# Retention's value and gate projections with 512 moving weight columns instead of 256, two heads to a tile

## The chip, the cores and the metric

One core of a Trainium2 chip runs the whole program. The metric is device time in microseconds (us), the median of the timed runs; lower is better. TensorE (PE in the profile) multiplies, VectorE (DVE), ScalarE (ACT) and GpSimd (POOL) do the elementwise work, and SyncE (SP) issues most of the transfers. Every engine takes its instructions in the order in which they were laid down; a waiting instruction holds up everything behind it on its engine.

## The reference

A trunk of four layers works on 384 token columns: 128 context tokens and 256 sample tokens, model width 1024. Layers 0 and 3 are S5 state-space layers, layer 1 is bidirectional retention, layer 2 is Hyena. The change is in layer 1:

```
proj = h @ w_in                       # h (L, 1024), w_in (1024, 6144)
q, k, v, gate = jnp.split(proj, [RET_QK, 2 * RET_QK, 2 * RET_QK + RET_V], axis=-1)
...                                   # 8 heads: q, k of 128, v and gate of 256 columns each
o = o * lax.rsqrt(jnp.mean(o * o, axis=-1, keepdims=True) + EPS)
out = (o.reshape(bsz, L, RET_V) * jax.nn.silu(gate.astype(F32))).astype(h.dtype) @ w_out
```

## The kernel before

**Split matmuls.** Every large projection is computed as three matmuls: both operands are split into a high and a low part (`hh`, `hl` of the activations, `wh`, `wl` of the weights), and `mm` (L135 to L139) adds hh·wh, hh·wl and hl·wh into one PSUM tile `psd`. There are three such tiles (pool `pd`), one PSUM bank of 512 float32 columns each. The weights come as slabs of 1 MB (tile `wr`, two buffers, `weight`, loaded by SP at L153) and are split piece by piece by `unit` (L157 to L165): ACT rounds a piece of 128x1024 to `wh` (L162), and DVE or POOL subtracts to get `wl` (L149 or L134; in retention every third piece goes to POOL). There are two buffers each of `wh` and `wl`. One such piece is called a unit below.

**Retention, layer 1.** It goes over four pairs of heads (`hp`). For a pair, q and k of both heads are projected with the weights stationary in the array and 384 token columns moving. Values v and gates g are projected the other way round by `tokmajor`: the activations (three blocks of 128 tokens, eight blocks of the model width) are stationary and 256 weight columns, one head's, move. A chunk (v or g of one head) is one slab, two units, 72 matmuls, and it accumulates in all three `psd` tiles at once, in the first 256 columns of each bank. When a token block is done, ACT copies v out of PSUM (L1084), or ACT and DVE make silu(g) (L531, L532). Between the chunks stand the parts of a head: `scores` (q·k, L1013 to L1024), `values` (L1029 to L1053: attention times v, the state, the norm, the product with the gate into `zt` at L1047, the new state) and `turn` (L1059: `zt` transposed for the output projection). `tick()` between them takes one piece of background work: tables for the S5 layer 3 (`gen_b1`, `gen_b2`, `gen_cs`: lines L629 to L676), which use DVE, POOL, PE, ACT and transfers.

**What sets the order.** The order on each engine is fixed before the run: the tile layer's scheduler takes the program's order and its own estimates and lays down one list per engine. A changed chunk therefore moves instructions on all engines and also, a little, in the layers behind it.

**Layer 3, at the end,** takes tables back from memory: `toeplitz` loads a tile `Tt` (two buffers) with eight transfers from SP (L850), PE transposes it (L855). SP's list also holds the loads of adaLN weights (`in_mod_w`) and of the GLU's weights (`in_s_w_glu`, L153), in the order laid down.

Of the kernel before, what the change touches and what calls it, by code (L numbers as in the profile page):

```python
# [10 lines left out]
F32 = mybir.dt.float32  # L11
# [6 lines left out]
D = 1024  # L18
NB = D // 128
# [11 lines left out]
DV = 256  # L31
# [74 lines left out]
def hybrid_trunk(ctx: ExitStack, tc: tile.TileContext, I, O, dbg=None, layers=(0, 1, 2, 3)):  # L106
    nc = tc.nc
    V, S, G, TE = nc.vector, nc.scalar, nc.gpsimd, nc.tensor
# [27 lines left out]
    def mm(out, lhs, rhs, start=True, stop=True):  # L136
        combos = [(0, 0)] if len(lhs) == 1 else [(0, 0), (0, 1), (1, 0)]
        for i, (a, b) in enumerate(combos):
            TE.matmul(out, lhs[a], rhs[b], start=start and i == 0, stop=stop and i == len(combos) - 1)  # L139
# [11 lines left out]
    def weight(src):  # L151
        raw = wraw.tile(list(src.shape), F32, tag="wr", name="wr")
        nc.sync.dma_start(raw, src)  # L153
        return raw

    def unit(ap):
        if not SPLIT:  # L157
            return [ap]
        a, b = ap.shape[1], ap.shape[2]
        hi, lo = [wsp.tile([128, 1024], F32R, tag="w" + q, name="w" + q)[:, :a * b].rearrange("p (a b) -> p a b", a=a)  # L160
                  for q in "hl"]
        S.copy(hi, ap)  # L162
        sub_any(lo, ap, hi.bitcast(F32))
        return [hi, lo]
# [20 lines left out]
                       k0 + kb == 0, k0 + kb == nkb - 1)  # L185
            epi(base + m, ps[:, :T])

    def tokmajor(raw, act, epi):
        pss = [psd() for _ in range(3)]
        for k0 in range(0, NB, 4):  # L190
            w = unit(raw[:, k0:k0 + 4, :])
            for t in range(3):
                for kb in range(4):
                    mm(pss[t][:, :256], [p[:, k0 + kb, t * 128:(t + 1) * 128] for p in act],
                       [p[:, kb, :] for p in w], k0 + kb == 0, k0 + kb == NB - 1)
        for t in range(3):
            epi(t, pss[t][:, :256])

    def dense(wsrc, nslab, act, nkb, epi, nt=1):
        for s in range(nslab):  # L200
# [152 lines left out]
    def tick(n=1):  # L353
        for _ in range(n):
            if bg:
                bg.popleft()()
# [172 lines left out]
    def silu2(out, ps):  # L529
        th = t384("silu")[:, :ps.shape[1]]  # L530
        S.activation(th, ps, AF.Tanh, scale=0.5)  # L531
        V.scalar_tensor_tensor(out, th, 1.0, ps, op0=OP.add, op1=OP.mult)  # L532
# [400 lines left out]
    def retention(i, zpool, hpool, nxt):  # L933
        es = ExitStack()
        pool = es.enter_context(tc.tile_pool(name="ret", bufs=1, reuse_waits="tile"))
        rot = es.enter_context(tc.tile_pool(name="retr", bufs=2, reuse_waits="tile"))
        h = adanorm(i, hpool)
# [10 lines left out]
        def t1(n):  # L948
            return pool.tile(sh1, F32, name=n)
        ax, e, w, w2, p, lg = t1("ax"), t1("le"), t1("lwq"), t1("lw2"), t1("lp"), t1("lg")  # L950
# [25 lines left out]
        W = I["ret_w_in"]  # L976
# [87 lines left out]
        for hp in range(4):  # L1064
            qk, vg = {}, {}
            heads = [head(2 * hp + m, m, qk, vg) for m in range(2)]

            def qk_chunk(nm, m, raw):
                def epi(_, ps):
                    o = rot.tile([128, T], F32, tag=nm + str(m), name=nm)  # L1070
                    r0 = 0 if nm == "q" else 2
                    sw = rot.tile([128, NLAT], F32, tag="rsw", name="rsw", bufs=1)
                    V.stream_shuffle(sw, ps[:, NCTX:T], [(q + 16) % 32 for q in range(32)])
                    V.tensor_mul(o[:, NCTX:], ps[:, NCTX:T], rope[:, r0, :])
                    S.activation(o[:, :NCTX], ps[:, :NCTX], AF.Copy, scale=1.0 if nm == "q" else 128 ** -0.5)  # L1075
                    gstt(sw, sw, rope[:, r0 + 1, :], OP.mult)
                    gstt(o[:, NCTX:], o[:, NCTX:], sw, OP.add)
                    qk[nm, m] = o
                firstmajor(i, raw[:, :, m * 128:(m + 1) * 128], h, epi, (0 if nm == "q" else 2) + m if hp == 0 else 9)

            def vg_chunk(nm, m):
                o = vg[nm, m] = rot.tile([128, 3, DV], F32, tag=nm, name=nm)
                tokmajor(weight(W[(8 if nm == "v" else 16) + 2 * hp + m]), h,
                         lambda t, ps: S.copy(o[:, t, :], ps) if nm == "v" else silu2(o[:, t, :], ps))  # L1084

            for n, sl in (("q", hp), ("k", 4 + hp)):
                raw = weight(W[sl])
                for m in range(2):
                    qk_chunk(n, m, raw)
                    if late:  # L1090
                        late.pop(0)()
                    tick()
            if hp == 0:
                z += [zblock(zpool, F32) for _ in range(16)]
            vg_chunk("v", 0)
            heads[0][0]()
            tick()
            vg_chunk("g", 0)
            heads[1][0]()
            tick()  # L1100
            vg_chunk("v", 1)
            heads[0][1]()
            tick()
            vg_chunk("g", 1)
            heads[0][2]()
            tick()
            late = [heads[1][1], heads[1][2]]
# [289 lines left out]
    hp = pool_of(eh, "hp")  # L1397
# [12 lines left out]
    for fb in range(NB):  # L1410
        t = xT[:, fb, :]
# [71 lines left out]
def _slabs(w, cols):  # L1483
    k, n = w.shape
    return w.reshape(k // 128, 128, n // cols, cols).transpose(2, 1, 0, 3)


def _layout(a):
    ca = np.ascontiguousarray
    o = {}  # L1490
    x = np.concatenate([a["x_prompt"][0], a["x_sample"][0]], 0)
    o["xT"] = x.T.reshape(NB, 128, T).transpose(1, 0, 2)
    o["condT"] = np.stack([a["c_ctx"], a["c"][0]]).reshape(2, NB, 128).transpose(2, 1, 0)
    o["vec"] = np.concatenate([
        a["mod_b"].reshape(-1, 128), a["norm_g"].reshape(-1, 128), a["final_g"].reshape(-1, 128),
        a["s5_b_glu"].reshape(-1, 128), a["hy_conv_w"].reshape(-1, 128), a["hy_conv_b"].reshape(-1, 128),
        a["hy_skip"].reshape(-1, 128)], 0).T
    o["mod_w"] = np.stack([_slabs(a["mod_w"][i], 256) for i in range(DEPTH)])

    def lanes(re, im):  # L1500
        v = np.stack([re, im], 0)
        v = v.reshape(2, 128, 4, 16, *v.shape[4:])
        return np.moveaxis(v, (2, 0, 3), (0, 1, 2)).reshape(128, 128, *v.shape[4:])
    lam, bc, h0, ds = [], [], [], []
    for j in range(2):
        lr, li = a["s5_lam_re"][j], a["s5_lam_im"][j]
        ls = np.broadcast_to(a["s5_log_step"][j].reshape(1, 128), (128, 128))
        lam.append(np.stack([lanes(lr, lr), lanes(li, li), ls], 1))
        br, bi = a["s5_b_re"][j], a["s5_b_im"][j]
        bl = np.stack([lanes(br, bi), lanes(bi, br)]).reshape(2, 128, 2, 16, 4, 16)  # L1510
        cr, ci = np.swapaxes(a["s5_c_re"][j], 2, 3), np.swapaxes(a["s5_c_im"][j], 2, 3)
        cl = np.stack([lanes(cr, ci), lanes(ci, cr)]).reshape(2, 128, 2, 16, 4, 16)
        v = np.stack([bl, cl]).reshape(2, 2, 128, 2, 4, 4, 4, 16)
        bc.append(v.transpose(4, 2, 5, 0, 3, 1, 6, 7))
        h0.append(lanes(a["state_s5"][0, j, :, 0], a["state_s5"][0, j, :, 1]))
        d = a["s5_d"][j].reshape(16, 4, 1, 16)
        ds.append(np.broadcast_to(d, (16, 4, 2, 16)).reshape(16, 128).T)
    o["s5lam"], o["s5bc"], o["s5h0"], o["s5d"] = map(np.stack, (lam, bc, h0, ds))
    wi = a["s5_w_in"]
    wi = np.concatenate([wi[..., :D].reshape(2, D, 8, 8, 16).swapaxes(3, 4).reshape(2, D, D), wi[..., D:]], 2)  # L1520
    o["s5_w_in"] = np.stack([_slabs(wi[j], 256) for j in range(2)])
    o["s5_w_glu"] = np.stack([_slabs(a["s5_w_glu"][j], 256) for j in range(2)])
    o["s5_w_out"] = np.stack([_slabs(a["s5_w_out"][j], 256) for j in range(2)])
    w = a["ret_w_in"][0]
    qk = w[:, :2 * D].reshape(D, 16, 2, 2, 2, 16).transpose(0, 1, 2, 4, 3, 5).reshape(D, 2 * D)
    o["ret_w_in"] = _slabs(np.concatenate([qk, w[:, 2 * D:]], 1), 256)
    o["ret_w_out"] = _slabs(a["ret_w_out"][0], 128)
    o["decay"] = np.concatenate([a["ret_decay_logit"][0].reshape(16, 1)] * 2, 0)
    s0 = a["state_ret"][0, 0].reshape(2, HEADS, 2, 2, 2, 16, DV).transpose(1, 2, 4, 3, 5, 0, 6)
    o["s0"] = s0.reshape(HEADS, 128, 2, DV)  # L1530
    o["hy_w_in"] = _slabs(a["hy_w_in"][0], 256)
    o["hy_w_out"] = _slabs(a["hy_w_out"][0], 128)
    o["hy_f_w1"], o["hy_f_w2"] = a["hy_f_w1"][0], a["hy_f_w2"][0]
    o["hy_f_b"] = np.stack([a["hy_f_b1"][0], a["hy_f_b2"][0]], 1)
    o["hy_f_w3"] = a["hy_f_w3"][0].reshape(64, 2, 2, 16, 128).transpose(3, 0, 2, 1, 4)
    return {k: ca(v) for k, v in o.items()}
# [39 lines left out]
```

## Time and profile before

| | |
|---|---|
| median of 3 runs | 1651.68 us (1649.26 to 1652.22) |
| the profiled execution's own time | 1654.23 us |
| its span from first to last instruction | 1652.1 us |
| PE busy | 1460.5 us, 88% of the span |
| DVE, ACT, POOL busy | 1250.0, 693.9, 663.5 us |
| mean granted TensorE clock | 0.942 |

Busy times are sums over instructions; a matmul's recorded duration includes its way through the array, so the distance between the starts of two matmuls is what a stream of them costs. "Idle before, releaser" in a row says how long the engine stood and what ended that.

### The profile page before, as it was taken

The numbers are of one execution on the slowest core, as the hardware profiler recorded it, in microseconds if no ns is written. First come the engines' busy times: TensorE is split into PE (matmuls) and PEld (weight loads), VectorE is DVE, ScalarE is ACT, GpSimd is POOL, SyncE is SP. The second block draws the span as 40 slices with busy tenths as digits, with TensorE's granted clock in tenths as the row PEclk, the third lists the DMA queues.
The fourth block names the chain that finished last, engine by engine and source line by source line (L and its number), as shares of the span: only waits on it lengthen the run. The fifth ranks groups of instructions, "written<-read, shape, count | busy, mean of one in ns | idle before, by whom it ended". The sixth has DMA issues, their size and how long they took to land. (4 is left out here: it accounts for less than half of the span.)

```text
span 1652.1 us, 27609 instructions
## 1 busy us (share of the span) xinstructions
PE 1460.5 (88%) x10370; PEld 1290.5 (78%) x10370; DVE 1250.0 (76%) x2935; ACT 693.9 (42%) x1275; POOL 663.5 (40%) x484
## 2 busy tenths in 40 slices
PE   5878876788689999999979999999999999998796
PEld 3655664577579888889968988989999798777686
DVE  8967996589787777755868988887888863399465
ACT  2444421234324333335445545445454442642453
POOL 2111331315275756551325665556656331131221
PEclk9788897799799999999979999999999999998898
DMA  8488589743645555544333223222321353675531
GB/s 355 137 269 243 144 213 272 223 147 140 229 160 182 183 204 188 186 146 142 129 106 102 97 77 99 100 77 77 105 96 66 132 227 140 191 206 179 167 128 64
DMA packets 107805, 261.39 MB, mean 158 GB/s; under 512 B 28535, under 2 KB 68568, under 8 KB 88088
## 3 DMA queue, kind: packets, MB, share of 16 engines
q1 hardware_dynamic: 80768, 200.12, 37.0%
q0 software_dynamic: 11984, 34.87, 7.6%
q10 hardware_dynamic: 14920, 24.65, 4.1%
q8 instruction: 82, 1.34, 0.3%
q14 instruction: 51, 0.42, 0.1%
HBM read 220.37 MB, written 30.83 MB: 152 GB/s over the span
## 5 line engine op out<-in xcount | busy, mean ns | idle before, releaser
L134 POOL TENSOR_TENSOR wl<-wr,wh 128x1024 fp32r<-128x1024 f32 (+2 forms) x99 | 249.7, 2524 | 313.3 <-ACT wh L162 286.2
L162 ACT CAST wh<-wr 128x1024 fp32r<-128x1024 f32 (+4 forms) x211 | 216.0, 1029 | 314.7 <-PE psd L139 222.3
L139 PE MATMUL psd<-hh,wh 128*128 128x384 f32 x880 | 305.0, 348 | 13.8 <-DVE X L796 5.1
L139 PE MATMUL psd<-hh,wl 128*128 128x384 f32 x880 | 303.4, 345 | 5.4 <-POOL wl L134 3.4
L139 PE MATMUL psd<-hl,wh 128*128 128x384 f32 x880 | 303.9, 345 | 2.7 <-DVE hl L470 2.5
L149 DVE TENSOR_TENSOR wl<-wr,wh 128x1024 fp32r<-128x1024 f32 (+3 forms) x112 | 146.7, 1311 | 72.8 <-ACT wh L162 70.3
L139 PEld LDWEIGHTS psd<-hh,wh 128*128 128x128 f32 x880 | 168.2, 192 | 26.2 <-issue 14.3
L139 PEld LDWEIGHTS psd<-hh,wl 128*128 128x128 f32 x880 | 168.3, 191 | 13.8 <-issue 5.1
L139 PEld LDWEIGHTS psd<-hl,wh 128*128 128x128 f32 x880 | 168.3, 191 | 12.4 <-issue 6.4
L139 PE MATMUL psd<-wh,hh 128*128 128x256 f32 x384 | 111.1, 293 | 3.9 <-ACT k L1075 1.8
L139 PE MATMUL psd<-wl,hh 128*128 128x256 f32 x384 | 110.7, 290 | 4.1 <-DVE wl L149 2.2
L139 PE MATMUL psd<-wh,hl 128*128 128x256 f32 x384 | 109.2, 286 | 0.0
L379 PE MATMUL psn<-wr,sgc 128*32 128x256 f32 x640 | 57.0, 449 | 30.7 <-DMA wr<-in_mod_w_dram 25.5
L630 DVE TENSOR_TENSOR xt<-BI,xc 128x512 f32<-128x512 f32 x52 | 47.2, 911 | 44.9 <-DMA CP<-xt 18.9
L139 PE MATMUL psd<-zb,wh 128*128 128x384 f32 x240 | 80.9, 338 | 0.0
L139 PEld LDWEIGHTS psd<-wl,hh 128*128 128x128 f32 x384 | 74.4, 194 | 6.2 <-DVE wl L149 3.1
L139 PEld LDWEIGHTS psd<-wh,hh 128*128 128x128 f32 x384 | 74.0, 194 | 6.1 <-ACT k L1075 2.3
L634 POOL TENSOR_TENSOR BP<-BP,xt 128x512 f32<-128x512 f32 x32 | 46.7, 1460 | 69.8 <-DVE xt L630 47.8
L139 PEld LDWEIGHTS psd<-wh,hl 128*128 128x128 f32 x384 | 74.4, 194 | 0.1
L630 DVE TENSOR_TENSOR xt<-FI,bc 128x512 f32<-128x512 f32 x64 | 51.8, 809 | 17.8 <-POOL BP L634 9.8
L632 POOL DMA_DIRECT2D CP<-xt x32 | 28.0, 929 | 92.7 <-DVE xt L630 43.6
L634 POOL TENSOR_TENSOR CP<-CP,xt 128x512 f32<-128x512 f32 x32 | 50.1, 1565 | 31.1 <-DVE xt L630 19.5
(385 smaller groups left out, 3890.4 us busy)
## 6 DMA issues: line engine op xcount, KB each, us to landing
wr<-in_mod_w_dram SPq DMA_DIRECT2D x40, 1024.0 KB
wr<-in_hy_w_in_dram SPq DMA_DIRECT2D x32, 1024.0 KB
wr<-in_ret_w_in_dram SPq DMA_DIRECT2D x24, 1024.0 KB
wr<-in_s_w_in_dram SPq DMA_DIRECT2D x16, 1024.0 KB
wm<-in_mod_w_dram SPq DMA_DIRECT2D x8, 1024.0 KB
CP<-xt POOLq DMA_DIRECT2D x32, 256.0 KB, 6.9
Tt<-scratch_kd_dram SPq DMA_DIRECT2D x128, 64.0 KB
wr<-in_s_w_glu_dram SPq DMA_DIRECT2D x8, 1024.0 KB
```

The costliest lines, as they stand in the source:

```text
L134: G.tensor_tensor(out, a, b, op=op)
L139: TE.matmul(out, lhs[a], rhs[b], start=start and i == 0, stop=stop and i == len(combos) - 1)
L149: V.tensor_sub(out, a, b)
L162: S.copy(hi, ap)
L379: TE.matmul(ps[q * 32:(q + 1) * 32, :256], sg[:, kb, 6 - 2 * u:38 - 2 * u], raw[:, kb, :], start=u == 0 and k2 == 0, stop=u == 3 and k2 == 1)
L630: eng.tensor_tensor(t, c2, x[:, 1].unsqueeze(2).to_broadcast([128, 4, 8, 16]), op=OP.mult)
L632: nc.gpsimd.dma_start(out, t, accum_op=OP.add)
L634: add.tensor_tensor(out, out, t, op=OP.add)
```

## The change

`tokmajor` now takes units of two blocks of the model width by 512 weight columns (instead of four by 256), loads its slab itself (half the depth of one 512-column slab, again 1 MB), and fills whole PSUM banks. `vg_chunk` is called once for v and once for g of a pair; its output tile holds both heads (one buffer of 512 columns instead of two of 256). v is copied out in one operation of 512 columns, the gate's silu stays in pieces of 256. The calls of `scores`, `values`, `turn` and `tick` are placed anew around the two chunks: v is projected for both heads before any gate. A host-side layout `ret_w_vg` holds the slabs of 512 columns.

```diff
-    def tokmajor(raw, act, epi):
+    def tokmajor(src, act, epi):
         pss = [psd() for _ in range(3)]
-        for k0 in range(0, NB, 4):
-            w = unit(raw[:, k0:k0 + 4, :])
+        for k0 in range(0, NB, 2):
+            if k0 % 4 == 0:
+                raw = weight(src[:, k0:k0 + 4, :])
+            w = unit(raw[:, k0 % 4:k0 % 4 + 2, :])
             for t in range(3):
-                for kb in range(4):
-                    mm(pss[t][:, :256], [p[:, k0 + kb, t * 128:(t + 1) * 128] for p in act],
+                for kb in range(2):
+                    mm(pss[t], [p[:, k0 + kb, t * 128:(t + 1) * 128] for p in act],
                        [p[:, kb, :] for p in w], k0 + kb == 0, k0 + kb == NB - 1)
         for t in range(3):
-            epi(t, pss[t][:, :256])
+            epi(t, pss[t])
...
-            def vg_chunk(nm, m):
-                o = vg[nm, m] = rot.tile([128, 3, DV], F32, tag=nm, name=nm)
-                tokmajor(weight(W[(8 if nm == "v" else 16) + 2 * hp + m]), h,
-                         lambda t, ps: S.copy(o[:, t, :], ps) if nm == "v" else silu2(o[:, t, :], ps))
+            def vg_chunk(nm):
+                o = rot.tile([128, 3, 2 * DV], F32, tag=nm, name=nm, bufs=1)
+                for m in range(2):
+                    vg[nm, m] = o[:, :, m * DV:(m + 1) * DV]
+
+                def epi(t, ps):
+                    if nm == "v":
+                        S.copy(o[:, t, :], ps)
+                        return
+                    for m in range(2):
+                        silu2(vg[nm, m][:, t, :], ps[:, m * DV:(m + 1) * DV])
+                tokmajor(I["ret_w_vg"][hp + (0 if nm == "v" else 4)], h, epi)
...
-            vg_chunk("v", 0)
             heads[0][0]()
+            vg_chunk("v")
             tick()
-            vg_chunk("g", 0)
             heads[1][0]()
             tick()
-            vg_chunk("v", 1)
+            vg_chunk("g")
             heads[0][1]()
             tick()
-            vg_chunk("g", 1)
             heads[0][2]()
             tick()
```

What the scheduler makes of it is shown at two places. The first is PE's list at the end of the last pair's gate chunk, just before the output projection begins (`zt` is the gated output of a head, `s_...` its cached state, `zhh` the first split input of the output projection). Before:

```order
L139 MATMUL psd<-wh,hl 128x256
L1059 MATMUL psm<-ident,zt 128x128 x5
L1029 MATMUL psm<-v,A 128x256
L1033 MATMUL psm<-s_7880,qf 128x256
L1034 MATMUL psm<-s_7880,qf 128x256
```

And with the change, at the same place:

```order
L139 MATMUL psd<-wh,hl 128x512
L139 MATMUL psd<-zhh,wh 128x384
L1061 MATMUL psm<-ident,zt 128x128 x2
L1031 MATMUL psm<-v,A 128x256
L1061 MATMUL psm<-ident,zt 128x128 x4
L1035 MATMUL psm<-s_7330,qf 128x256
```

The transposes of the pair's first head stood behind a gate that had been ready one chunk earlier; now they stand one or two matmuls behind the last matmul of the gate chunk that makes their gate.

The second place is SP's list in layer 3 (`Tt` are the tables of `toeplitz`, eight transfers a table; `wr` are weight slabs). Before:

```order
L153 DMA wr<-in_mod_w_dram 128x2048
L850 DMA Tt<-scratch_kd_dram 16x8x128 x5
L153 DMA wr<-in_s_w_glu_dram 128x2048 x2
L850 DMA Tt<-scratch_kd_dram 16x8x128 x16
L153 DMA wr<-in_s_w_glu_dram 128x2048 x2
```

And with the change:

```order
L153 DMA wr<-in_mod_w_dram 128x2048
L852 DMA Tt<-scratch_kd_dram 16x8x128
L153 DMA wr<-in_s_w_glu_dram 128x2048
L852 DMA Tt<-scratch_kd_dram 16x8x128 x8
L153 DMA wr<-in_s_w_glu_dram 128x2048
L852 DMA Tt<-scratch_kd_dram 16x8x128 x16
```

The first of the two GLU slabs that stood right before the last two tables (the sixteen transfers) has moved ahead of the table before them.

## Rows read from the trace of the kernel before

**Rows 1.** The page's first line.

```profile
span 1652.1 us, 27609 instructions
```

**Rows 2.** Retention's stage: PE, PEld, DVE, ACT, POOL busy us (instructions); clock; DMA share; GB/s.

```profile
470.00:765.00 295.00, 276.18 (x2055) 255.57 (x2056) 207.48 (x369) 111.38 (x249) 172.06 (x127) 0.98 0.52 176
```

**Rows 3.** Groups of matmuls, retention: one of three alike forms (wl,hh and wh,hl too).

```profile
L139 PE MATMUL psd<-wh,hh 128*128 128x256 f32 x384 | 111.1, 293 | 3.9 <-ACT k L1075 1.8 <-ACT q L1075 1.4 <-DVE g L532 0.7
```

**Rows 4.** PE's waits, 465 to 765 us: total us, times, longest; six of twelve.

```profile
PE psd L139 <- POOL wl L134: 4.1, 5, 1.2
...
PE psd L139 <- DVE g L532: 2.9, 3, 2.2
PE psd L139 <- DVE wl L149: 2.2, 3, 1.0
...
PE psd L139 <- ACT k L1075: 1.8, 2, 0.9
...
PE psm L1059 <- DVE zt L1047: 1.1, 1, 1.1
...
PE psm L1021 <- ACT PB L673: 0.2, 1, 0.2
```

**Rows 5.** PE's timeline inside a chunk: 256 columns, full clock, 68 starts apart.

```profile
741.10 0.28 PE L139 MATMUL psd<-wh,hh 128*128 128x256 f32 x1
...
749.26 0.28 PE L139 MATMUL psd<-wh,hl 128*128 128x256 f32 x1
```

**Rows 6.** PE's timeline in layer 3: 384 columns, full clock, 12 starts apart.

```profile
1584.77 0.33 PE L139 MATMUL psd<-gh,wh 128*128 128x384 f32 x1
...
1586.85 0.33 PE L139 MATMUL psd<-gh,wh 128*128 128x384 f32 x1
```

**Rows 7.** A stretch of low clock (columns as Rows 2), and 256-column starts, nine apart.

```profile
471.00:477.80 6.80, 5.91 (x29) 5.62 (x28) 4.98 (x7) 0.28 (x1) 5.34 (x5) 0.50 0.39 124
...
474.59 0.41 PE L139 MATMUL psd<-wh,hh 128*128 128x256 f32 x1
...
476.51 0.41 PE L139 MATMUL psd<-wh,hh 128*128 128x256 f32 x1
```

**Rows 8.** Groups of ACT, POOL and DVE work, 465 to 765 us.

```profile
L162 ACT CAST wh<-wr 128x1024 fp32r<-128x1024 f32 x45 | 47.2, 1050 | 65.8 <-PE psd L139 54.0 <-DVE nr L279 4.9 <-DVE xt L630 2.4
...
L673 ACT COPY PB<-psm 128x512 f32<-128x512 f32 x28 | 15.6, 593 | 14.0 <-PE psd L139 5.6 <-DVE xt L630 4.1 <-PE psm L672 3.7
L1084 ACT COPY v<-psd 128x256 f32<-128x256 f32 x24 | 8.7, 371 | 17.2 <-PE psd L139 16.4 <-POOL CP L634 0.6 <-issue 0.2
...
L134 POOL TENSOR_TENSOR wl<-wr,wh 128x1024 fp32r<-128x1024 f32 x15 | 37.2, 2480 | 31.8 <-ACT wh L162 31.8
...
L149 DVE TENSOR_TENSOR wl<-wr,wh 128x1024 fp32r<-128x1024 f32 x30 | 42.3, 1410 | 9.5 <-ACT wh L162 9.3
...
L532 DVE SCALAR_TENSOR_TENSOR g<-silu,psd 128x256 f32<-128x256 f32 x24 | 9.5, 413 | 7.2 <-ACT silu L531 7.2
```

**Rows 9.** Timelines of PE and DVE where one pair's gate chunk meets the next pair.

```profile
603.98 0.59 PE L139 MATMUL psd<-hh,wh 128*128 128x384 f32 x1 [2.17 <-DVE g L532]
...
599.40 3.59 DVE L629 TENSOR_TENSOR CP<-B,xc 128x512 f32<-128x512 f32 x2 [1.09 <-DMA scratch_cpd_dram<-CP]
```

**Rows 10.** The chain that ended last, two of its longest pieces: start, us, what.

```profile
1528.71 10.38 DMA Tt<-scratch_kd_dram
1543.01 6.49 DMA Tt<-scratch_kd_dram
```

**Rows 11.** SP's timeline in layer 3.

```profile
1514.46 7.87 SPq L850 DMA_DIRECT2D Tt<-scratch_kd_dram  x5
1522.43 3.10 SPq L153 DMA_DIRECT2D wr<-in_s_w_glu_dram  x2
1526.81 16.79 SPq L850 DMA_DIRECT2D Tt<-scratch_kd_dram  x16
```

**Rows 12.** Layer 3 while the last tables load (columns as Rows 2).

```profile
1525.00:1530.00 5.00, 3.86 (x48) 3.50 (x44) 2.72 (x13) 3.09 (x6) 1.05 (x2) 1.00 1.01 406
```

More of the change, by code (lines that the diff above doesn't have):

```diff
@@ L1525, in _layout @@
     qk = w[:, :2 * D].reshape(D, 16, 2, 2, 2, 16).transpose(0, 1, 2, 4, 3, 5).reshape(D, 2 * D)
-    o["ret_w_in"] = _slabs(np.concatenate([qk, w[:, 2 * D:]], 1), 256)
+    o["ret_w_in"] = _slabs(qk, 256)
+    o["ret_w_vg"] = _slabs(w[:, 2 * D:], 512)
     o["ret_w_out"] = _slabs(a["ret_w_out"][0], 128)
```

## The prediction

> **What bounds the kernel now.** I read the stages first. The layers run one after another, so a microsecond taken from the stage of retention comes off the span [rows 1] unless a later stage waits for something else. In that stage, 295 us long, PE is busy for 276 us, DVE for 207, POOL for 172 and ACT for 111, at a granted clock of 0.98 and with half of the DMA share unused [rows 2]. PE is the bound. The waits of PE confirm it from the other side: the twelve rows of that list add up to 20.3 us, none of them above 4.1 us in total [rows 4]. So what shortens PE's stream shortens the stage, and what can take it back is a wait of PE for a weight part (`wl`), for a PSUM tile that is not yet read out (g, k), or for `zt`.
>
> The stream itself I read from the distances between starts, since recorded durations overlap (293 ns for a 256-column matmul [rows 3] that in fact comes every 120 ns). At full clock, 256 columns: 749.26 - 741.10 = 8.16 us over 68 steps, 120.0 ns each [rows 5]. 384 columns: 2.08 us over 12 steps, 173.3 ns [rows 6]. The 128 columns between them cost 53.3 ns, 0.417 ns a column, which is one column per cycle at 2.4 GHz; what is left is 13.3 ns at 256 columns and 13.3 ns at 384. So a matmul costs its columns and a fixed 13.3 ns. At a clock of 0.50 the fixed part is gone: 1.92 us over nine steps is 213.3 ns, 256 cycles of 1.2 GHz and nothing more [rows 7].
>
> **The change, part by part.**
>
> *The stream.* 3 x 384 = 1152 matmuls of 256 columns [rows 3] become 576 of 512. The columns stay; 576 fixed parts go. No row has 512 columns, so the price of one is drawn along the line of the two rows: 213.3 + 13.3 = 226.7 ns. Some 30 of the 1152 run at low clock, where nothing is saved. 561 x 13.3 ns = **-7.5 us**. Bounds: 0, if 512 columns cost twice what 256 cost (240 ns), and -7.7, if all run at full clock. I take the line because the two rows have the same remainder. The weight loads that go with the 576 lie beside the matmuls and are not counted again.
>
> The Trainium skill, page "TensorE: Matmul & The Clock Gate", section "Wait — 56ns, not 53.3ns?", gives a matmul N/2.4 GHz plus about 2.5 ns when warm; by it the 576 would be worth about 1.4 us, an estimate from that page. The rows here show 13.3 ns and not 2.5, so the trace does not agree.
>
> *The units.* Their number (eight a pair), size and split between DVE and POOL stay. But a unit now lasts 18 x 226.7 ns = 4.08 us on PE instead of 36 x 120.0 = 4.32 us. With two buffers, the unit after next is prepared while one unit runs: 1.05 us of rounding on ACT and 1.41 us on DVE or 2.48 us on POOL [rows 8], 2.5 or 3.5 us without any queue. A DVE unit keeps 1.6 us in hand, a POOL unit 0.55 us, and POOL and DVE also carry the background tables in order. Eight times before, PE waited for `wl` (4.1 us for POOL's, 2.2 us for DVE's) [rows 4]. A unit that is waited for loses its whole 0.24 us. Bounds: 0, and 32 x 0.24 = 7.7 us if every unit is limited by its preparation. I take six units in the stage, **+1.5 us**, because PE's waits for `wl` are few.
>
> *The ends of chunks.* ACT's v copies become 12 of 512 columns; the row for a 512-column copy out of PSUM is 593 ns, against 2 x 371 [rows 8]. That is off the path: with the token blocks outermost in a unit, block 0 is complete 12 x 226.7 ns = 2.7 us before the chunk's end, and its copy is done by then. A gate block now needs two tanh and two products of 413 ns on DVE [rows 8] instead of one before its PSUM tile is free, and the next pair's q chunk takes that tile. Before, PE stood 2.17 us there once, because DVE's list had two background products (3.59 us, they themselves waited for a transfer) ahead of the gate [rows 9]; three such waits cost 2.9 us [rows 4]. Chunk ends fall from four a pair to two, but the one in front of q stays, with one product more. Bounds: -2.9 us if these waits vanish, +1.7 us if all four pairs wait one product more. I take **+0.5 us**.
>
> *The last pair.* PE's list now has the first head's transposes one or two matmuls behind the last gate matmul. They wait for tanh, product and `zt`. The nearest row is the one wait for `zt`, 1.1 us [rows 4]; I take **+1.1 us**, with 0 and 2.2 as bounds (once or twice). Behind it stand the second head's products and the output projection, all on PE. For the other pairs, the q and k chunks stand between, which hide it.
>
> *Layer 3.* Nothing was changed there, but SP's list was. At the end the chain runs through two table loads of 10.38 and 6.49 us [rows 10], issued at 1526.81 us right behind two GLU slabs (2 MB) [rows 11], while the DMA share is 1.01 at 406 GB/s [rows 12]. With the change one slab goes out a table earlier. If it has landed by then, 1 MB at 406 GB/s, 2.6 us, is taken from the queue in front of the tables: -2.6 us. Against it: the eight transfers of the table before now stand between the two slabs. In the group of five before, 7.87 us passed [rows 11], 1.57 us each; if these eight can only start where the first slab stood and go at that rate, the last tables start 12.6 us later: +12.6 us is the other bound. I take **-1.0 us**. The moved rows in Hyena I cost at nothing, without a row that bounds them.
>
> **Sum:** -7.5 + 1.5 + 0.5 + 1.1 - 1.0 = -5.4 us. Against the profiled execution's own 1654.2 us (span 1652.1 us) that is 1648.8 us; its time lies 2.5 us above the median of the runs shown, so against the median of 1651.7 us it is **1646 us**.
>
> **The rivals.**
>
> 1. *More than the stream.* The gate waits vanish (-2.9) and the slab leaves the table loads' way (-2.6), with the unit and `zt` terms near nothing: -7.5 - 5.5 = -13.0, 1638.7 us. For it speaks that half of the chunk ends go; against it that the waits for g came from background work on DVE, which stays.
>
> 2. *The gain is eaten.* PE's stream is shorter, but the preparation of units sets the pace. 32 units that all lose 0.24 us give +7.7 - 7.5, about 1652 us. The same time comes out if the fixed part does not belong to the matmul as such and 512 columns cost 240 ns. For the first speaks that POOL units have only 0.55 us in hand; against it that PE's waits for `wl` were 6.3 us in 295. Against the second speaks the equal remainder of the two rows. The page's 2.5 ns, named above, would end here too.
>
> 3. *Slower, through SP's list in layer 3.* The eight transfers between the slabs start late and go at 1.57 us each, which pushes the last two tables back by 12.6 us, and these end the chain: -7.5 + 1.5 + 0.5 + 1.1 + 12.6 = +8.2, 1659.9 us. It decides once the last tables start more than 7.7 us later, counted from the end of retention (4.4 us to use up the gain, 3.3 to be seen). For it speaks that these transfers wait for one another and for PE today; against it that the slab in front of them is free to go early.
>
> **How the numbers follow.** About 0.2%, 3.3 us, is what a measurement of this kernel can tell from no change. Forecast (3.3 to 9 us faster): 0.47. First rival (over 9 us faster): 0.18. Second (within 3.3 us): 0.21. Third (slower by over 3.3 us, with other new orders that I have not priced): 0.14. So faster 0.65, same 0.21, slower 0.14. The forecast's own range is 1642.5 to 1648.5 us. All bounds together reach from -13.2 us (1638.5) to +16.7 us (1668.4); the lower end stays, and above I cut where the second rival's bound (+4.1 with the other terms at their upper ends but layer 3's) is still held: 1638 to 1656 us.
>
> **What would show it.** The starts of 512-column matmuls at full clock should be 226.7 ns apart; 240 ns would break the first term. Retention's stage should be some 4 to 7 us shorter at the same clock. PE's waits for `wl` should come to some 8 us (6.3 + 1.5). At the end of the last gate chunk PE should show a wait for `zt` of 1 to 2 us. The two table loads in the chain's end should together take less than 16.9 us, and start at the same distance from the end of retention. The prediction is wrong if the stage is shorter by less than 3 us, or if layers 2 and 3 change by more than 3 us.

## The result and the profile after

The changed kernel is slower. Its median is 1670.16 us (1668.57 to 1672.48) beside 1651.05 us (1649.26 to 1652.22) for the kernel before, a ratio of 1.0106 with a 95% interval of 1.0086 to 1.0127, so 14 to 21 us. The profiled execution took 1672.48 us; its page begins:

```profile
span 1670.7 us, 26436 instructions
```

Beside [rows 1] that is 18.6 us more with 1173 instructions fewer. I cut the span at events that both kernels have. In the table, a stage runs from the start of the first v matmul (or g, where g comes first) to the start of the last matmul of the v and g chunks; "behind" is the way from there to the first matmul of Hyena I, layer 2; "rest" is the way from there to the end. A second execution of each kernel (e16 and e13 below) shows how far the pieces repeat.

| profiled execution | first v matmul at | stage | behind | rest | span |
|---|---|---|---|---|---|
| before | 469.3 | 289.5 | 89.8 | 803.5 | 1652.1 |
| before again (e16) | 475.0 | 289.3 | 90.4 | 801.3 | 1655.9 |
| after | 471.7 | 291.6 | 101.7 | 805.8 | 1670.7 |
| after again (e13) | 468.5 | 290.0 | 102.7 | 807.1 | 1668.2 |

Two things went wrong. The stage is not shorter (290.8 us on average beside 289.4; the two executions of after differ by 1.6 us), and 12 us are lost behind it. Some 4 us more stand in the rest, half of them behind the last matmul of layer 3's input projection and half ahead of it. No experiment here isolates these 4 us: in the other versions below, the rest lies between 799.6 and 806.9 us, in those with all four pairs wide between 799.6 and 804.4.

First what came as forecast. PE's timeline inside a chunk, 512 columns, 12 starts apart, answers to [rows 5]:

```profile
750.11 0.39 PE L139 MATMUL psd<-wh,hh 128*128 128x512 f32 x1
...
752.83 0.39 PE L139 MATMUL psd<-wh,hl 128*128 128x512 f32 x1
```

2.72 us over 12 steps is 226.7 ns. The window of retention's stage has the columns of [rows 2]; behind it stand PE's waits from 467 to 767 us, four of fifteen, as in [rows 4]:

```profile
470.00:765.00 295.00, 268.72 (x1449) 217.06 (x1447) 208.81 (x346) 105.30 (x221) 175.82 (x129) 0.98 0.53 176
```

```profile
PE psd L139 <- DVE wl L149: 7.5, 7, 3.4
PE psm L674 <- DVE nr L282: 3.0, 1, 3.0
...
PE psd L139 <- DVE g L534: 2.0, 2, 1.7
...
PE psd L139 <- POOL wl L134: 1.6, 1, 1.6
```

PE is busy for 7.5 us less than in [rows 2], but that is not the stage's own difference: before, the window ends with 6 us of full work behind the stage, after, with PE standing. Between the first and the last start of the chunks PE is busy for 267.6 us after (267.2 in e13) beside 270.4 before (267.5 in e16), and idle for 24.0 us (22.8) beside 19.1 (21.7). So most of the stream's gain is used up while PE is busy, and the waits grow. The waits for `wl` are 9.1 us in place of 6.3, 7.5 of them now for DVE, the longest 3.4 us.

Now the end of the last gate chunk. PE's timeline, with what ended its idle time in brackets:

```profile
763.23 0.39 PE L139 MATMUL psd<-wh,hl 128*128 128x512 f32 x1
764.00 0.45 PE L139 MATMUL psd<-zhh,wh 128*128 128x384 f32 x1 [0.38 <-ACT zhh L245]
773.47 0.69 PE L1061 MATMUL psm<-ident,zt 128*128 128x128 f32 x2 [9.03 <-DVE zt L1049]
773.95 1.06 PE L1031 MATMUL psm<-v,A 128*128 128x256 f32 x2
774.80 1.06 PE L1061 MATMUL psm<-ident,zt 128*128 128x128 f32 x4
...
776.83 0.59 PE L1037 MATMUL psm<-v,A 128*128 128x256 f32 x2
777.26 0.59 PE L1038 MATMUL psm<-v,A 128*128 128x256 f32 x2
...
780.09 0.52 PE L139 MATMUL psd<-zb,wh 128*128 128x384 f32 x1
```

One matmul of the output projection runs, then PE stands for 9.03 us before head 6's transposes; head 7's products are next in the list. What it waits for is seen on ACT and then on DVE:

```profile
763.43 2.16 ACT L245 CAST zhh<-zb 128x384 fp32r<-128x384 f32 x5 [0.51 <-PE psd L139]
765.50 0.64 ACT L533 ACTIVATE silu<-psd 128x256 f32<-128x256 f32 x2
766.04 1.33 ACT L245 CAST zhh<-zb 128x384 fp32r<-128x384 f32 x3
767.27 1.75 ACT L245 CAST zhl<-zb 128x384 fp32r<-128x384 f32 x4
768.92 0.83 ACT L162 CAST wh<-wr 128x768 fp32r<-128x768 f32 x1
769.65 0.38 ACT L533 ACTIVATE silu<-psd 128x256 f32<-128x256 f32 x1
769.92 0.38 ACT L1043 ACTIVATE junk<-psm 128x256 f32<-128x256 f32 x1
```

```profile
770.66 0.41 DVE L534 SCALAR_TENSOR_TENSOR g<-silu,psd 128x256 f32<-128x256 f32 x1
771.15 0.17 DVE L1044 TENSOR_SCALAR rss<-rss 128x3 f32<-128x3 f32 x1
...
772.74 0.16 DVE L286 SCALAR_TENSOR_TENSOR rrs<-nr 128x3 f32<-128x3 f32 x1
772.93 1.27 DVE L1049 SCALAR_TENSOR_TENSOR zt<-psm,rrs,g 128x256 f32<-128x256 f32 x3
```

ACT rounds z for the output projection between the tanhs (12 casts, then a weight cast), so the last tanh starts 6.4 us behind the chunk's last start. Head 6's norm stands behind that tanh on ACT (`junk`) and DVE (`rss` to `rrs`), and only then comes `zt`. PE stands, the granted clock falls to its low level, 0.50, and head 6's transposes and the first of head 7's products run at it: the two products at 773.95 us take 0.85 us to the next start, two later ones (776.83 us) 0.43. Windows of after, columns as [rows 2]:

```profile
760.00:765.00 5.00, 4.07 (x17) 2.84 (x16) 1.78 (x5) 3.20 (x8) 1.95 (x2) 1.00 0.15 52
765.00:770.00 5.00, 0.00 (x0) 0.00 (x0) 0.97 (x3) 5.00 (x14) 0.00 (x0) 0.60 0.00 0
770.00:775.00 5.00, 1.53 (x5) 1.24 (x6) 4.61 (x16) 1.12 (x7) 0.00 (x0) 0.50 0.20 56
775.00:780.00 5.00, 5.00 (x24) 4.47 (x23) 5.00 (x12) 2.54 (x9) 0.00 (x0) 0.87 0.00 0
```

The projection's matmuls run in a row from 780.1 us, 16.9 us behind the last gate matmul. Before, PE was busy throughout from 755 to 790 us at a clock of 1.00, and the distance was 4.4 us. The last gate matmul, the first of the projection, and a window of before:

```profile
758.86 0.29 PE L139 MATMUL psd<-wh,hl 128*128 128x256 f32 x1
...
763.23 0.52 PE L139 MATMUL psd<-zhh,wh 128*128 128x384 f32 x1
```

```profile
760.00:765.00 5.00, 5.00 (x27) 4.59 (x26) 4.99 (x12) 5.00 (x13) 0.00 (x0) 1.00 0.00 0
```

### The profile page after: what moved, and what is told of

Its sections match the earlier page's. It is cut to its first block, busy times and chain, and to the rows that moved or that the text cites. A ratio compares the mean times of both kernels' runs of the same rounds, so it can differ in the third digit from the quotient of the medians.

```text
span 1670.7 us, 26436 instructions
## 1 busy us (share of the span) xinstructions
PE 1455.5 (87%) x9794; PEld 1257.8 (75%) x9794; DVE 1250.0 (75%) x2935; ACT 693.0 (41%) x1263; POOL 669.9 (40%) x484
## 5 line engine op out<-in xcount | busy, mean ns | idle before, releaser
L149 DVE TENSOR_TENSOR wl<-wr,wh 128x1024 fp32r<-128x1024 f32 (+3 forms) x112 | 143.3, 1280 | 72.2 <-ACT wh L162 68.1
L632 DVE TENSOR_TENSOR xt<-BI,xc 128x512 f32<-128x512 f32 x52 | 53.1, 1023 | 42.7 <-POOL CP L636 18.1
L139 PE MATMUL psd<-wl,hh 128*128 128x512 f32 x192 | 79.6, 415 | 5.1 <-DVE wl L149 3.3
L636 POOL TENSOR_TENSOR BP<-BP,xt 128x512 f32<-128x512 f32 x32 | 52.3, 1636 | 65.0 <-DVE xt L632 49.6
L139 PE MATMUL psd<-wh,hl 128*128 128x512 f32 x192 | 76.2, 397 | 0.0
L139 PE MATMUL psd<-wh,hh 128*128 128x512 f32 x192 | 72.6, 411 | 3.1 <-ACT q L1077 1.4
L631 DVE TENSOR_TENSOR BP<-F,bc 128x512 f32<-128x512 f32 x64 | 59.5, 939 | 12.9 <-PE psm L674 10.8
L631 DVE TENSOR_TENSOR CP<-B,xc 128x512 f32<-128x512 f32 x52 | 43.9, 879 | 24.0 <-DMA scratch_cpd_dram<-CP 14.3
L797 DVE TENSOR_TENSOR X<-X,m 128x64 f32<-128x64 f32 x184 | 60.5, 329 | 0.0
L381 PEld LDWEIGHTS psn<-wr,sgc 128*32 128x32 f32 x640 | 19.1, 119 | 54.9 <-DMA wr<-in_mod_w_dram 29.3
```

The source lines that it names most:

```text
L149: V.tensor_sub(out, a, b)
L381: TE.matmul(ps[q * 32:(q + 1) * 32, :256], sg[:, kb, 6 - 2 * u:38 - 2 * u], raw[:, kb, :], start=u == 0 and k2 == 0, stop=u == 3 and k2 == 1)
L631: eng.tensor_tensor(out, c1, x[:, 0].unsqueeze(2).to_broadcast([128, 4, 8, 16]), op=OP.mult)
L632: eng.tensor_tensor(t, c2, x[:, 1].unsqueeze(2).to_broadcast([128, 4, 8, 16]), op=OP.mult)
L636: add.tensor_tensor(out, out, t, op=OP.add)
L797: V.tensor_add(dst, dst, m1[:, 0])
```

## The experiments

Single runs of one kernel spread over up to some 20 us in these comparisons, so beside each ratio I give the stage and "behind" of its profiled execution. Each ratio is to runs of the kernel before that were taken beside it; their medians lie between 1651.5 and 1656.4 us. Theory A names the last gate chunk's end, B the width and background work in the stage, C the list of SP in layer 3 (my third rival). `vg_chunk1` is the chunk of before, one head and 256 columns, but it reads half of a 512-column slab and writes into one tile for both heads.

**Only the last pair old (e1).** The calls, shown joined here, stand on lines of their own.

```diff
+            if hp < 3:
...
+            else:
+                vg_chunk1("v", 0); heads[0][0](); tick()
+                vg_chunk1("g", 0); heads[1][0](); tick()
+                vg_chunk1("v", 1); heads[0][1](); tick()
+                vg_chunk1("g", 1); heads[0][2](); tick()
```

> The changed kernel with only the last of the four pairs done as before: four chunks of 256 columns, v and g of the first head, then v and g of the second. Theory A (the last gate: both heads' gates are now complete only at the end of the last chunk, ACT's last tanh stands behind the rounding for the output projection, and PE's list waits for it): 12.8 us of the 19 come back, 1657 us. Theory B (512 columns slow the stage itself, by units that are waited for and by background work that now falls in bunches between fewer chunks): a quarter of it at most, some 2 us, 1668 us. Theory C (SP's list in layer 3, as my third rival said): no change, 1670 us.

Measured: 1655.75 us, ratio to before 1.0028 (1.0007 to 1.0049); stage 292.5, behind 93.2 us. Theory A holds for what is behind the stage: 9 of the 12 us are back. The three wide pairs that stay bring no gain.

**The counterpart: only the last pair new (e10).** The two branches of e1 exchanged.

> The counterpart of the run with only the last pair old: the first three pairs as before (256 columns, old order), only the last pair with 512 columns and both heads' gates last. Theory A (the end of the last gate chunk): the distance from the last gate matmul to the first matmul of Hyena I is some 12 us longer than before (about 102 instead of 90 us), and the whole 1660 to 1665 us. Theory B (the width within the stage): 1651 to 1654 us.

Measured: 1671.38 us, ratio 1.0102 (1.0073 to 1.0130); stage 287.4, behind 104.7 us. The one pair costs as much as the whole change, 18 us by the medians; 1660 to 1665 us was expected. Its stage is 2.0 us shorter than before, so one wide pair at the end loses nothing within the stage. Its wait for `zt` is that of after:

```profile
PE psm L1072 <- DVE zt L1060: 9.0, 1, 9.0
```

**ACT's rounding behind the last tanh (e2).**

```diff
-        S.activation(th, ps, AF.Tanh, scale=0.5)
+        lastg[0] = S.activation(th, ps, AF.Tanh, scale=0.5)
...
-        op.split(0, 14)
+        with tc.issue_after(lastg[0].ins):
+            op.split(0, 14)
```

> The changed kernel with one edge more: on ACT the rounding for the output projection may not stand ahead of the last tanh of the last gate. Theory A: the last tanh ends at about 764.5 us instead of 770, so the 17.3 us between the last gate matmul and the output projection become some 10 to 12 (the norm's chain and zt still stand between, 4 us), 1663 to 1666 us. If instead the order on ACT does not matter, because the rounding that is moved back is then waited for just as long: 1669 to 1671 us. Theories B and C: no change, 1670 us.

Measured: 1668.39 us, ratio 1.0097 (1.0075 to 1.0120); stage 290.0, behind 98.2 us. The last tanh starts 4 us earlier, at 765.6 us, and 3.5 us come back behind the chunk; the median, 1.8 us lower than that of after, lies within the spread and between the two ranges expected. PE's waits there, 756 to 785 us:

```profile
PE psd L139 <- ACT zhh L245: 4.5, 1, 4.5
PE psm L1063 <- DVE zt L1051: 1.2, 1, 1.2
```

PE now waits for the rounding, which stands behind tanh and norm, and then for `zt`. ACT's order is a part of the loss; moving it alone mostly exchanges one wait for another.

**The norm early as well (e12).**

`values()` is cut in two: `products()`, with the norm, which is entry 3 of a head and is called half way through the last gate chunk, and `zt` behind the chunk.

```diff
-            vg_chunk("g")
+            vg_chunk("g", heads[0][3] if hp == 3 else lambda: None)
...
+        with tc.issue_after(lastg[0].ins):
+            op.split(0, 14)
```

> The changed kernel, in the last pair with the first head's products and norm in the middle of the gate chunk, and on ACT no rounding for the output projection ahead of the last tanh. Between the last gate matmul and the first head's transposes only tanh, product and zt are left. Theory A in its full form (what waits is the chain tanh, product, norm, zt, wherever ACT's rounding stands): the wait for zt falls from 9.0 to about 3 us, the distance from the last gate matmul to Hyena I to 93 to 96 us, 1660 to 1664 us. If that time is lost wherever both heads end together: no change, 1668 to 1671 us.

Measured: 1657.36 us, ratio 1.0028 (1.0004 to 1.0052); stage 291.3, behind 93.1 us, so 9 of the 12 us are back, with both heads' gates still last; that is more than the 1660 to 1664 us expected. On ACT the last tanh now starts at 763.98 us, and on PE the wait has nearly gone:

```profile
764.40 0.44 PE L1070 MATMUL psm<-ident,zt 128*128 128x128 f32 x2 [0.64 <-DVE zt L1064]
```

```profile
765.00:770.00 5.00, 5.00 (x27) 4.61 (x26) 5.00 (x12) 5.00 (x14) 0.00 (x0) 1.00 0.18 52
```

PE stays busy at a clock of 1.00 where it stood at 0.60 in after. So it is the serial chain tanh, product, norm, `zt`, put behind the last chunk together with ACT's rounding, and not the width, that costs the 9 us. The norm early without the change on ACT was not run, so beyond e2's 3.5 us the two shares are not separated.

**The order without the width (e4).** `vg_chunk1("v", 0)` and `("v", 1)` at the place of the wide v chunk, g likewise; matmuls and units of 256 columns.

> The changed kernel's order and pair tiles (v of both heads, then g of both heads, background work and head work at the same places), but with matmuls of 256 columns and units of 4 x 256 as before. If the order is the cause (theory A and the bunches of theory B): the loss stays and the 7.5 us of the stream go too, 1672 to 1678 us. If the width is the cause (units of 512 columns that are waited for): back to 1651 to 1656 us.

Measured: 1669.76 us, ratio 1.0112 (1.0079 to 1.0146); stage 293.0, behind 96.7 us. By the median the loss stays without the width, a little under the lower end that was expected, so the order is enough for a loss. But the profiled execution was the fastest of its runs (1659.45 us), and it shows only 6.7 of the 12 us behind the stage. There the first head's gate is complete one chunk of 256 columns earlier, ACT has two casts ahead of the last tanh in place of twelve, and PE's wait is shorter:

```profile
PE psm L1072 <- DVE zt L1060: 3.5, 1, 3.5
```

Its stage is 3.6 us longer than before, with 5.1 us of waits for ACT's copies of v, where two v chunks now follow each other.

**g first (e6), and g first with all head work later (e9).**

```diff
-            vg_chunk("v")
+            vg_chunk("g")
...
-            vg_chunk("g")
+            vg_chunk("v")
```

In e9, also `values` and `turn` of the first head go to the next pair's q and k chunks, and in the last pair `op.part(0, 0, 8)` stands between products and transposes.

> The changed kernel with the two chunks of a pair exchanged: g of both heads first, then v of both. Theory A (the last gate): no tanh is left at the end of the last chunk; in its place the first head's products wait for the last copy of v, and its norm and zt follow (about 6 us). From the last matmul of the chunks to the output projection some 8 to 11 us instead of 16.9: 1661 to 1665 us. If any chunk that both heads need last costs the same, whichever it is: 1669 to 1671 us.

> The changed kernel with g first, and all work of both heads behind the chunks moved into the next pair's q and k chunks; in the last pair, a part of the output projection stands between the first head's products and its transposes. If order alone costs the time behind the last chunk, PE finds work there and the projection starts some 6 us behind the chunk: 1653 to 1658 us, and below 1651 if the q and k chunks also lose their waits. If the width costs it: no better than 1665 us.

Measured: e6 1669.69 us, 1.0116 (1.0082 to 1.0151), stage 293.8, behind 102.9 us; e9 1668.64 us, 1.0086 (1.0054 to 1.0118), stage 288.7, behind 104.2 us. Both miss what theory A gave; by its expectation e9 would speak for the width as the cause, against which e12 stands. In e6, the first head's products stand behind the chunk now; no tanh is late, but norm and `zt` follow the products: PE waits 5.1 us for `zt`, again at a clock of 0.50 (770 to 775 us). In e9 that wait is gone and the projection starts 2.6 us behind the chunk, but its other waits (2.8 us for `wl`, 1.2 for `zhl`, 0.9 for POOL's `wl`) and the head work that was moved there stand in "behind", which is no shorter; how the 14 us share between them is not shown. So exchanging v and g does not help: in e6 another chain of both heads waits at the last chunk's end.

**Background work spread in the wide chunks (e5).** A slot in the middle of each chunk, one behind it.

> The changed kernel with the four slots of background work per pair spread as before, one to each half of a 512-column chunk and one behind each chunk's end, instead of two together behind each chunk. The last pair's order stays. If the bunches of background work cause the 8.6 us that the q and k chunks of the second to fourth pairs lost: 1661 to 1663 us. If they do not: 1669 to 1671 us.

Measured: 1668.0 us, ratio 1.0106 (1.0080 to 1.0132); stage 291.6, behind 102.6 us. Spreading the slots gains nothing that shows; other waits took the place of those in after (7.3 us for g on DVE).

**Background tables ahead of the stage (e8 with 256 columns, e7 with 512).** All their matmuls stand ahead of the first q chunk on PE:

```diff
+        drain()
+        hold = ExitStack()
+        hold.enter_context(tc.issue_after(lastbg[0].ins))
         late, z = [], []
         for hp in range(4):
```

> The kernel before (256 columns, old order), with all background tables of retention put on PE ahead of the first q chunk, so that the stage of the v and g chunks runs without them. The whole gets longer, since the tables then stand alone: 1670 to 1720 us. What counts is the distance from the first v matmul to the last gate matmul beside the same kernel with 512 columns. Ideal streams of the two differ by 7.9 us.

> The changed kernel with the same move of the background tables ahead of the first q chunk. If waits for work that shares DVE, ACT and POOL with the background tables ate the gain of the stream: the distance from the first v matmul to the last gate matmul is 6 to 9 us shorter than in the kernel before with the same move. If 512 columns are slow by themselves, or the units are: less than 3 us shorter. The wait behind the last gate chunk (17 us to the output projection) stays, since nothing of it is changed.

Measured: e8 1753.17 us (more than expected) and e7 1764.17 us in all, 1.0608 (1.0565 to 1.0650) and 1.0681 (1.0643 to 1.0719). The stage without tables, e8 and then e7:

```profile
622.70:857.00 234.30, 234.30 (x1685) 229.31 (x1684) 90.97 (x215) 82.32 (x165) 68.98 (x54) 1.00 0.39 127
```

```profile
627.00:856.70 229.70, 229.70 (x1111) 199.31 (x1110) 96.94 (x201) 78.29 (x145) 72.22 (x55) 1.00 0.41 129
```

PE is busy throughout in both, and the wide stage is 4.8 us shorter (234.5 and 229.7 us between the first and last matmul): less than the 6 to 9 expected, more than nothing. Behind it, 102.2 us stand beside 91.7. So the width does win time where PE never waits; with the tables in the stage this gain is not seen.

**Only v wide (e11).** g keeps two chunks of 256 columns, head work about where it stood before.

> Only v is projected for two heads at once with 512 columns; g keeps its two chunks of 256 columns, and head work stands where it did before. Half of the stream's gain (3.9 us) is left to be won. Theory A: the end of the last chunk costs nothing here (about 90 us to Hyena I). If background work does not eat the rest, 1647 to 1650 us; if it does, 1651 to 1654 us.

Measured: 1659.36 us, ratio 1.0028 (1.0007 to 1.0049); stage 291.8, behind 94.6 us. Even this half brings nothing: it is slower than both ranges expected, with no late gate behind the stage.

**The norm early in all pairs (e14), and everything spread over half chunks (e15).**

> As the run with the norm early in the last pair, but in all four pairs the first head's products and norm stand in the middle of the gate chunk. If the stage's new waits come from head work that now falls together behind the gate chunk, the stage is 3 to 5 us shorter than 291 us and the whole 1651 to 1654 us. If they come from the background tables, or any order has them: no change against the run with the last pair alone, 1656 to 1659 us.

> The same, and the second head's scores and one slot of background work in the middle of the v chunk, one in the middle of the gate chunk, so that every half chunk of 512 columns has what a chunk of 256 columns had before. If the places of head and background work ate the stream's gain: the stage 284 to 287 us, the whole 1648 to 1652 us. If the waits stay wherever the work stands: stage 290 to 292 us, the whole 1656 to 1659 us.

Measured: e14 1669.06 us, 1.0062 (1.0038 to 1.0086), stage 299.4 us at a granted clock of 0.94, behind 95.3 us; e15 1659.61 us, 1.0016 (0.9997 to 1.0035), stage 291.7, behind 95.0 us. In e14, above both ranges expected, PE waited 8.3 us for `zt` before transposes and 5.5 us more for `zt` before a table's matmuls. e15 came out close to what was expected for waits that stay wherever the work stands. No place that I tried for head and background work beside the tables made the stage with four wide pairs clearly shorter than before; the shortest, e9 with 288.7 us, had the last pair's head work moved out of it.

**Both kernels again (e13, e16).**

> The changed kernel unchanged, beside the other three on one chip, since runs of one kernel spread over some 10 us: 1668 to 1672 us, with 101 to 103 us from the last gate matmul to Hyena I.

> The kernel before, unchanged: 1650 to 1655 us. The stage of the v and g chunks, 289.5 us in the profiled execution of before, should come out within 1 us if its length repeats; if it comes out at 292 or more, the stage did get shorter with the change, and the execution of before was a lucky one.

Measured: after 1670.40 us, 1.0101 (1.0077 to 1.0125); before 1656.09 us, 0.9995 (0.9976 to 1.0015). The stage of before repeats within 0.2 us, that of after within 1.6 us, "behind" of either kernel within 1 us. The time of e16 lies 1.1 us above its expected range. No version ran faster than the kernel before.

## Why the prediction was wrong

**The last pair (+1.1 us, bounds 0 and 2.2) is the step that failed.** It measured +12 us behind the chunk, 9.0 us of them PE's wait for `zt`. I saw in PE's list that head 6's transposes stand right behind the last gate matmul, and priced the wait with the nearest wait for `zt`. That row comes from inside the stage, where matmuls of other chunks cover most of this chain and no rounding for the output projection stands on ACT. I did not go through ACT's list, where the last tanh stands behind twelve casts and a weight cast (6.1 us by the rows of after), nor ask where the norm would stand. The chain on the path was casts, tanh, product, norm, `zt`, and low clock behind it. e1 and e10 put the loss in this pair, e12 in this chain, and e4 shows part of it without the width. Of the 12 us, e1, e11 and e12 leave 3 to 4.5; where these go is open.

**The stream (-7.5 us): the mechanism was right, the size a little off.** The median pace is 226.7 ns as drawn. The mean over all matmuls at pace is 229.2 ns for 512 columns and 119.8 for 256, so 576 matmuls save 239.6 - 229.2 = 10.4 ns each, 6.0 us. The Trainium skill, page "TensorE: Matmul & The Clock Gate", section "Wait — 56ns, not 53.3ns?", gives about 2.5 ns beyond N/2.4 GHz. The 226.7 - 213.3 = 13.4 ns here, where each matmul has a weight load of its own, do not agree with that either.

**Units (+1.5) and chunk ends (+0.5) were too small for a stage whose engines share work.** Of the 6 us nothing is left. PE's waits for `wl` in the stage are 9.1 us in after and 8.4 in e13, beside 6.3 in [rows 4] and 7.4 in e16: 1 to 3 us more, within the bound of 7.7; the gate waits fell by about 1 us. To see all of it I sorted the distances between starts in the stage, as means of two executions of each kernel. The q, k, v and g matmuls at pace give 6.0 us back. Distances 0.05 to 0.22 us over the pace (matmuls right behind float32 work, short waits, low clock) grew from 11.0 to 15.4 us, longer ones from 19.7 to 22.6 us; of these, those in the q and k chunks, to which I gave no term, went from 4.9 to 9.1 us. The float32 matmuls with their gaps add 0.3 us. The sum is -6.0 + 4.4 + 2.9 + 0.3 = +1.6 us, beside +1.4 measured. The second rival named the outcome for the stage, the gain eaten, but its mechanism, waits for prepared units, covers at most 3 of the 7.3 us; e7 and e8 show that the gain is there without the background tables. Which queue decides I could not settle: e5, e14 and e15 move the waits, none removes them.

**Layer 3 (-1.0) had the wrong sign, but no great size.** From the last matmul of layer 3's input projection to the end, the two executions of after took 142.3 and 142.2 us beside 140.7 and 139.9 before, so about +2. The slab did go out a table earlier, but the last tables did not come sooner:

```profile
1539.61 4.67 SPq L852 DMA_DIRECT2D Tt<-scratch_kd_dram  x5
1545.19 0.33 SPq L153 DMA_DIRECT2D wr<-in_s_w_glu_dram  x1
1546.14 15.35 SPq L852 DMA_DIRECT2D Tt<-scratch_kd_dram  x16
```

The sixteen table issues of [rows 11] started 15.4 us behind that matmul before (1526.81 - 1511.4) and 17.7 us after (1546.14 - 1528.4). Counted from the first matmul of Hyena I, where retention ends, they started 3.1 us later (5.7 between e16 and e13). Both are below the 7.7 us at which the third rival decides, so the slower side came true by another mechanism than the one I named for it. The two table loads in the chain's end did get shorter together, as the sign said (13.6 us beside 16.9 in [rows 10]), but in that chain a GLU slab now stands between them:

```profile
1537.69 7.43 DMA Tt<-scratch_kd_dram
1545.19 10.33 DMA wr<-in_s_w_glu_dram
...
1560.89 6.15 DMA Tt<-scratch_kd_dram
```

The signs by which the prediction was to be judged said so in the right places: the stage was not shorter by 3 us, the wait for `zt` was 9 us instead of 1 to 2, and layers 2 and 3 changed by 4 us. One sum of the prediction is not what its words say: "all bounds together", +16.7 us, leaves the stream at -7.5 us; with the stream's own bound of 0 it is +24.2 us.

## What to carry to other kernels

When two independent chains are merged into one wide step, ask what each of them used to do while the other ran: the first head's gate and norm had been made beside the second head's chunk, so that its transposes found `zt` ready. Price the wait at the end of the merged step by walking the list of every engine on its chain, not by the nearest wait of the same name. And a shorter stream of the busiest engine need not shorten its stage when other work shares the engines; see whether the gain is there at all by taking the shared work out of the stage, as e7 and e8 do.

## What the hardware showed

A float32r matmul (the type of the split weights) that follows a float32 one is slow here. PE's timeline of after, the first and second 512-column matmul behind a head's float32 products:

```profile
749.21 0.59 PE L1035 MATMUL psm<-s,qf 128*128 128x256 f32 x2
749.46 0.58 PE L139 MATMUL psd<-wl,hh 128*128 128x512 f32 x1
749.88 0.40 PE L139 MATMUL psd<-wh,hl 128*128 128x512 f32 x1
```

The next start comes after 0.42 us instead of 0.227. Worked out from the starts of all v, g, q and k matmuls in the stage, behind a switch (waits above 0.2 us left out, and only where another of these matmuls follows): 56 cases cost 6.3 us over their pace before, 64 cost 8.0 us after, some 120 ns each (v and g alone: 29 and 47 cases, 3.4 and 6.3 us); in e7, without tables, 36 cost 6.8 us, 190 ns each. The single values lie near 85, 110 and 190 ns; what decides between them is not shown. So how often the order switches between the two kinds on PE has a price of its own.
